# Attention outputs kept token-major in split fp32r, divided by the row sums on the way out of PSUM, and transposed afterwards

## The chip, the cores and the metric

One core of a Trainium2 chip runs the whole kernel. The metric is the device time in microseconds (us) of one execution, lower is better. The engines named below are TensorE (PE; its weight loads are shown apart as PEld), VectorE (DVE), ScalarE (ACT), GpSimd (POOL) and SyncE (SP), which issues most transfers.

## What is computed

One decoder block on 512 tokens of width 2048 in float32. Attention (16 heads of 64) and a state-space group share one input projection; each output is normalised, the two are concatenated and projected, and an MLP follows. With 512 tokens and key blocks of 256, every query sees all its past, so attention is plain causal attention with a distance penalty.

```python
h = rms_norm(x, norm1_gain)
q, k, v, u = split(h @ w_in)                    # 1024 columns each
attn = softmax(rms(q) @ rms(k).T * scale - slope * dist, causal) @ v
ssm = glu(gelu(s5(u)))
mixed = concat([rms_norm(attn, attn_out_gain), rms_norm(ssm, ssm_out_gain)])
x = x + mixed @ w_out
x = x + relu(rms_norm(x) @ w_ff1) ** 2 @ w_ff2
```

## The kernel before, in words

Every large product is made in fp32r (a float32 matmul that reads each operand once and at reduced precision), with both operands split into a high and a low part, so that it takes three matmuls: low by high, high by low, high by high. `panel` (lines 132 to 138) makes 512 columns: for each 128 rows of the weights, `split_w` makes the two parts of the weights (ACT copies the high part at line 110, DVE subtracts at line 111), and twelve matmuls of 512 columns go to four PSUM banks named `mm`. There is one set of four `mm` banks, so that the first matmul of a panel waits until the bank has been read out.

The stages follow one another in the program: the state-space part with its projection, q, k and v of heads 0 to 7, `attention(0)`, q, k and v of heads 8 to 15, `attention(1)`, two panels with `w_glu` (operand names `sh`, `sl`), four panels with the lower half of `w_out` (`zh`, `zl`, called the z panels below; their results are added to `x` at line 803), four panels with its upper half (`ah`, `al`, the a panels), and the MLP. The order on each engine is not the program's: a scheduler at build time places every instruction by priority and by its own estimate of times, and hands out buffers. Each engine then works through its list strictly in that order. So the pieces of `attention` stand between panel matmuls on PE, where the scheduler put them.

`attention` handles two heads at a time (`pr`), and for each of four query blocks `i` of 128 tokens and each head `e` one step, 64 steps in all:

- two matmuls make scores in the bank `sps` (lines 701, 702), of 128, 256, 384 or 512 columns for i = 0 to 3;
- DVE adds the distance term, takes the minimum and writes `sm` (line 706); ACT takes the exponential and the row sum (line 709); DVE inverts the sum (line 711) and POOL multiplies the probabilities by it (line 712);
- i + 1 transposes with `ident` put the probabilities into the bank `pps` (line 715), and ACT copies them to `pt` (line 717), in float32;
- i + 1 products in plain float32 (line 722) with 64 columns of `vv` as weights and 128 columns of `pt` moving; they fill `ops`, one head in its upper and one in its lower 64 partitions, so that the output stands feature by token. A float32 product of this kind appears in the trace as two instructions.

`sps`, `pps` and `ops` have one bank each. ACT copies `ops` to `oraw` once for each pair (line 726). Before the a panels, `oraw` is split into `ah`, `al` (lines 186, 187), its squares are made on ACT (line 816) and summed on POOL (line 817), and four small matmuls (line 779) add them over the partitions.

Of the kernel before, what the change touches and what calls it, by code (L numbers as in the profile page):

```python
# [8 lines left out]
F32 = mybir.dt.float32  # L9
F32R = mybir.dt.float32r  # L10
# [7 lines left out]
P = 128  # L18
# [3 lines left out]
DH = 64  # L22
# [23 lines left out]
def hybrid_block_kernel(ctx, tc, x, norm1_gain, w_in, q_norm_gain, k_norm_gain,  # L46
# [137 lines left out]
    def scaled_split(dh, dl, src, gain):  # L184

        S.activation(dh, src, AF.Copy, scale=gain)
        V.scalar_tensor_tensor(dl, src, gain, dh.bitcast(F32), op0=ALU.mult, op1=ALU.subtract)
# [498 lines left out]
        V.tensor_sub(klo[e][own], k, khh[own].bitcast(F32))  # L686
        return qhl, khh

    def attention(hf, qT, kT, vv, oraw):

        for pr in range(4):
            oT = aux("ops", "ops")
            slope = [2.0 ** (-8.0 * (hf * 8 + 2 * pr + e + 1) / H) for e in range(2)]
            parts = [head_parts(qT, kT, pr, e, 1.0 / slope[e]) for e in range(2)]
            for i in range(4):
                n = (i + 1) * P
                pts = []
                for e in range(2):
                    qhl, khh = parts[e]
                    sps = aux("sps", "sps")  # L700
                    PE.matmul(sps[:, :n], qhl[:, i * P:(i + 1) * P], khh[:, 0:n], start=True, stop=False)
                    PE.matmul(sps[:, :n], qhl[:, i * P:(i + 1) * P], klo[e][:, 0:n], start=False, stop=True)
                    sm = ap_.tile([P, 512], F32, name="sm", tag="sm", bufs=3)

                    mn = small.tile([P, 1], F32, name="mn", tag="mn")
                    V.tensor_tensor_reduce(sm[:, :n], sps[:, :n], dist[:, 512 - n:512], slope[e], 3e38,
                                           op0=ALU.add, op1=ALU.min, accum_out=mn)
                    rsum = small.tile([P, 1], F32, name="rsum", tag="rsum")
# [9 lines left out]
                    pts.append(pt)  # L718

                for b in range(i + 1):  # L720
                    for e in range(2):
# [6 lines left out]
    oraw = [ap_.tile([P, 4, 512], F32, name="oraw0")]  # L728
    attention(0, *qkv0, oraw[0])
    qkv1 = qkv(1, lambda n: ap_.tile([P, 4, 512], F32, name=n + "1"))  # L730


    sh, sl = [], []
# [6 lines left out]
            V.tensor_copy(h_, s0t(k))  # L740
            V.tensor_sub(l_, s0t(k), h_.bitcast(F32))

    oraw.append(page("oraw1"))
    attention(1, *qkv1, oraw[1])

    def sact(k):
        return sh[k // 4][:, k % 4, :], sl[k // 4][:, k % 4, :]
# [58 lines left out]
    open_banks(early, tx=3)  # L806
    ah = [page("ah0", F32R), page("ah1", F32R)]
    al = [page("al0", F32R), page("al1", F32R)]
    for k in range(8):
        o = oraw[k // 4][:, k % 4, :]  # L810
        scaled_split(ah[k // 4][:, k % 4, :], al[k // 4][:, k % 4, :], o, ga[:, k:k + 1])
        if k == 0:
            S.activation(rbc, o, AF.Square)
        else:
            oq = t2("oq")
            S.activation(oq, o, AF.Square)
            G.tensor_add(rbc, rbc, oq)
    rstda = row_rstd(rbc, "a")
    fin.close()

    def aact(k):
# [13 lines left out]
    for n in range(4):  # L835
        ps = panel(w_out, 0, 8, n * 512, aact, True)
        for m in range(4):
            with hi():
                xs = x1[m][:, n * 512:(n + 1) * 512]
                V.scalar_tensor_tensor(xs, ps[m], rstda[:, 2 * m:2 * m + 1], xs, op0=ALU.mult, op1=ALU.add)  # L840
# [240 lines left out]
```

## Time and profile before

| | |
|---|---|
| median of 3 runs | 2099.13 us (2098.68 to 2099.46) |
| the profiled execution | 2096.33 us, span of its instructions 2094.5 us |
| PE busy | 2061.8 us, 98% of the span |
| DVE, ACT, POOL busy | 1534.4, 829.1, 80.5 us |
| mean granted PE clock | 0.995 of full speed |

The profile covers one execution, from its first to its last instruction. A start-to-start distance of two PE rows is what an instruction costs PE when nothing is waited for; the duration that a row gives is longer, since matmuls overlap.

### The profile page before, as it was taken

The numbers are of one execution on the slowest core, as the hardware profiler recorded it, in microseconds if no ns is written. First come the engines' busy times: TensorE is split into PE (matmuls) and PEld (weight loads), VectorE is DVE, ScalarE is ACT, GpSimd is POOL, SyncE is SP. The second block draws the span as 40 slices with busy tenths as digits, with TensorE's granted clock in tenths as the row PEclk, the third lists the DMA queues.
The fourth block names the chain that finished last, engine by engine and source line by source line (L and its number), as shares of the span: only waits on it lengthen the run. The fifth ranks groups of instructions, "written<-read, shape, count | busy, mean of one in ns | idle before, by whom it ended". The sixth has DMA issues, their size and how long they took to land.

```text
span 2094.5 us, 26148 instructions
## 1 busy us (share of the span) xinstructions
PE 2061.8 (98%) x9881; PEld 1672.2 (80%) x9881; DVE 1534.4 (73%) x2659; ACT 829.1 (40%) x1349; POOL 80.5 (4%) x122
## 2 busy tenths in 40 slices
PE   8999999999999999999999999999999999999998
PEld 6777777776777888888888888888888888888887
DVE  6999994564773546677777777776877777777767
ACT  5244544455644333333333333333333333333332
POOL 1100000111331000000000000000000000000000
PEclk9999999999999999999999999999999999999999
DMA  6343332221233412333233333333333323333332
GB/s 194 119 124 96 93 101 81 79 73 61 82 110 105 162 37 69 117 105 98 93 111 101 101 114 108 94 97 111 101 101 111 110 91 100 111 101 101 109 108 95
DMA packets 149614, 213.51 MB, mean 102 GB/s; under 512 B 15672, under 2 KB 82320, under 8 KB 148976
## 3 DMA queue, kind: packets, MB, share of 16 engines
q1 hardware_dynamic: 136240, 201.36, 30.5%
q10 hardware_dynamic: 12416, 8.92, 1.4%
q0 software_dynamic: 832, 1.57, 0.3%
q8 instruction: 78, 1.28, 0.3%
q14 instruction: 48, 0.39, 0.1%
HBM read 204.54 MB, written 7.27 MB: 101 GB/s over the span
## 4 chain that ended last, share of the span: by engine, by line
PE 93%; DVE 5%; DMA 1%; ACT 1%; issue 1%; SPq 0%; POOL 0%; DVEq 0%; ACTq 0%; POOLq 0%
PE f L887 11%; PE f L888 11%; PE f L889 11%; PE g L983 9%; PE g L985 9%; PE g L981 9%; PE mm L132 7%; PE mm L133 7%; PE mm L134 7%; PE ops L722 1%; PE mm L136 1%; PE mm L138 1%; PE mm L137 1%; DMA x<-in_x_dram 1%; PE pps L715 1%; DVE wl L111 1%
## 5 line engine op out<-in xcount | busy, mean ns | idle before, releaser
L868 ACT CAST th<-w 128x1024 fp32r<-128x1024 f32 x349 | 361.7, 1053 | 642.6 <-PE g L985 467.4
L991 DVE TENSOR_TENSOR x<-x,g 128x512 f32<-128x512 f32 x434 | 293.6, 683 | 241.7 <-PE g L985 241.1
L869 DVE TENSOR_TENSOR tl<-w,th 128x1024 fp32r<-128x1024 f32 x349 | 425.6, 1220 | 61.1 <-ACT th L868 61.0
L887 PE MATMUL f<-h2h,tl 128*128 128x512 f32 x1024 | 398.6, 389 | 0.0
L888 PE MATMUL f<-h2l,th 128*128 128x512 f32 x1024 | 398.5, 389 | 0.0
L889 PE MATMUL f<-h2h,th 128*128 128x512 f32 x1024 | 398.4, 389 | 0.0
L983 PE MATMUL g<-tl,lf 128*128 128x512 f32 x868 | 337.9, 389 | 0.4 <-DVE tl L869 0.4
L985 PE MATMUL g<-th,lf 128*128 128x512 f32 x868 | 337.7, 389 | 0.0
L981 PE MATMUL g<-th,lf 128*128 128x512 f32 x868 | 320.0, 389 | 0.0
L889 PEld LDWEIGHTS f<-h2h,th 128*128 128x128 f32 x1024 | 192.2, 188 | 40.0
L887 PEld LDWEIGHTS f<-h2h,tl 128*128 128x128 f32 x1024 | 192.2, 188 | 39.9
L888 PEld LDWEIGHTS f<-h2l,th 128*128 128x128 f32 x1024 | 192.2, 188 | 39.8
L111 DVE TENSOR_TENSOR wl<-raw,wh 128x512 fp32r<-128x512 f32 x208 | 147.6, 711 | 96.8 <-ACT wh L110 96.2
L110 ACT CAST wh<-raw 128x512 fp32r<-128x512 f32 x208 | 127.8, 619 | 194.2 <-PE mm L134 117.3
L983 PEld LDWEIGHTS g<-tl,lf 128*128 128x128 f32 x868 | 162.9, 188 | 35.0 <-DVE tl L869 1.2
L981 PEld LDWEIGHTS g<-th,lf 128*128 128x128 f32 x868 | 162.9, 188 | 33.9
L985 PEld LDWEIGHTS g<-th,lf 128*128 128x128 f32 x868 | 162.9, 188 | 33.8
L133 PE MATMUL mm<-wl,xh 128*128 128x512 f32 x384 | 152.4, 397 | 0.0
L134 PE MATMUL mm<-wh,xh 128*128 128x512 f32 x384 | 152.1, 397 | 0.0
L132 PE MATMUL mm<-wh,xl 128*128 128x512 f32 x384 | 150.8, 399 | 0.7 <-ACT qs L628 0.4
L896 ACT ACTIVATE r<-r 128x512 f32<-128x512 f32 x64 | 40.0, 627 | 146.5 <-DVE r L895 146.5
L132 PEld LDWEIGHTS mm<-wh,xl 128*128 128x128 f32 x384 | 72.2, 188 | 16.6 <-issue 1.6
(350 smaller groups left out, 2552.4 us busy)
## 6 DMA issues: line engine op xcount, KB each, us to landing
w<-in_w_ff_dram SPq DMA_DIRECT2D x256, 512.0 KB, 3.8
raw<-in_w_in_dram SPq DMA_DIRECT2D x64, 512.0 KB, 3.7
raw<-in_w_out_dram SPq DMA_DIRECT2D x32, 512.0 KB, 3.6
x<-in_x_dram SPq DMA_DIRECT2D x7, 1024.0 KB, 10.3
m<-kp ACTq DMA_DIRECT2D x16, 256.0 KB, 3.3
raw<-in_w_glu_dram SPq DMA_DIRECT2D x8, 512.0 KB, 3.6
out_dram<-x SPq DMA_DIRECT2D x16, 256.0 KB, 2.2
ud<-sy ACTq DMA_DIRECT2D x8, 256.0 KB, 2.0
```

The source lines that it names most:

```text
L132: PE.matmul(ps[m], xl[:, ms], wh, start=st, stop=False)
L133: PE.matmul(ps[m], xh[:, ms], wl, start=False, stop=False)
L134: PE.matmul(ps[m], xh[:, ms], wh, start=False, stop=sp)
L868: S.copy(th, src)
L869: V.tensor_sub(tl, src, th.bitcast(F32))
L887: PE.matmul(ps[m], wl[:, k % 4, ms], xh_, start=k == 0, stop=False)
L888: PE.matmul(ps[m], wh[:, k % 4, ms], xl_, start=False, stop=False)
L889: PE.matmul(ps[m], wh[:, k % 4, ms], xh_, start=False, stop=k == 15)
L981: PE.matmul(ps[t], al_, th[:, q, :], start=first and q == 0, stop=False, skip_group_check=True)
L983: PE.matmul(ps[t], ah_, tl[:, q, :], start=False, stop=False, skip_group_check=True)
L985: PE.matmul(ps[t], ah_, th[:, q, :], start=False, stop=q == 1, skip_group_check=True)
L991: V.tensor_add(xs, xs, ps[t])
```

## The change: what it does

The products of probabilities and values change sides. The transposed probabilities become the weights (128 by 128) and the values move, so that the output stands token by feature. Both are split for fp32r: `pth`, `ptl` from the transposed probabilities (ACT copies, DVE subtracts), and `vhl`, which holds for each head the 64 high and the 64 low columns of the values side by side. Each product is then two matmuls: `pth` by all 128 columns, and `ptl` by the 64 high ones. The two halves are added when `ops` is read out, for two query blocks at a time, by three DVE operations that also multiply by the inverted row sums; the division by them before the transposes (POOL) is gone. The squares for the norm are taken on ACT with a row sum, and 32 transposes (`ot`), in the banks that `sps`, `pps` and `ops` leave, give the feature-by-token layout that the a panels need.

```diff
-    def attention(hf, qT, kT, vv, oraw):
+    def attention(hf, qT, kT, vv, o_sb):
...
+            vhl = ap_.tile([P, 4, 2, 2, DH], F32R, name="vhl", tag="vhl", bufs=1)
+            v = vv[:, :, pr * P:(pr + 1) * P].rearrange("p b (e d) -> p b e d", e=2)
+            S.copy(vhl[:, :, :, 0, :], v)
+            V.tensor_sub(vhl[:, :, :, 1, :], v, vhl[:, :, :, 0, :].bitcast(F32))
+            rsum = small.tile([P, 4, 2], F32, name="rsum", tag="rsum")
...
-                    S.activation(sm[:, :n], sm[:, :n], AF.Exp, bias=mn, scale=-1.0, accum_out=rsum)
-                    rinv = small.tile([P, 1], F32, name="rinv", tag="rinv")
-                    V.reciprocal(rinv, rsum)
-                    G.tensor_scalar(sm[:, :n], sm[:, :n], rinv, 0.0, op0=ALU.mult, op1=ALU.add)
+                    S.activation(sm[:, :n], sm[:, :n], AF.Exp, bias=mn, scale=-1.0,
+                                 accum_out=rsum[:, i, e:e + 1])
                     pps = aux("pps", "pps")
                     for b in range(i + 1):
                         PE.transpose(pps[:, b * P:(b + 1) * P], sm[:, b * P:(b + 1) * P], ident)
-                    pt = ap_.tile([P, 512], F32, name="pt", tag="pt", bufs=3)
-                    S.copy(pt[:, :n], pps[:, :n])
...
-                        PE.matmul(oT[e * DH:(e + 1) * DH, i * P:(i + 1) * P],
-                                  vv[:, b, pr * P + e * DH:pr * P + (e + 1) * DH],
-                                  pts[e][:, b * P:(b + 1) * P], start=b == 0, stop=b == i)
-            with hi():
-                S.copy(oraw[:, pr, :], oT)
+                    S.copy(pth[:, :n], pps[:, :n])
+                    V.tensor_sub(ptl[:, :n], pps[:, :n], pth[:, :n].bitcast(F32))
+                    o = ops[:, i % 2, e]
+                    for b in range(i + 1):
+                        bs = slice(b * P, (b + 1) * P)
+                        PE.matmul(o.rearrange("p l d -> p (l d)"), pth[:, bs],
+                                  vhl[:, b, e].rearrange("p l d -> p (l d)"), start=b == 0, stop=False,
+                                  skip_group_check=True)
+                        PE.matmul(o[:, 0], ptl[:, bs], vhl[:, b, e, 0], start=False, stop=b == i,
+                                  skip_group_check=True)
+                if i % 2:
+                    with hi():
+                        rinv = small.tile([P, 2, 2], F32, name="rinv", tag="rinv")
+                        V.reciprocal(rinv, rsum[:, i - 1:i + 1])
+                        d = o_sb[:, i - 1:i + 1, pr * P:(pr + 1) * P].rearrange("p i (e d) -> p i e d", e=2)
+                        V.tensor_copy(d, ops[:, :, :, 0])
+                        V.tensor_add(d, d, ops[:, :, :, 1])
+                        V.tensor_mul(d, d, bc(rinv, 3, DH))
...
-    qkv1 = qkv(1, lambda n: ap_.tile([P, 4, 512], F32, name=n + "1"))
+    qkv1 = qkv(1, lambda n: page(n) if n == "vv" else ap_.tile([P, 4, 512], F32, name=n + "1"))
...
+    for e in range(2):
+        for i in range(4):
+            junk = t2("junk")
+            S.activation(junk, o_sb[e][:, i, :], AF.Square, accum_out=ssa[:, i, e:e + 1])
...
     for k in range(8):
-        o = oraw[k // 4][:, k % 4, :]
-        scaled_split(ah[k // 4][:, k % 4, :], al[k // 4][:, k % 4, :], o, ga[:, k:k + 1])
...
-            G.tensor_add(rbc, rbc, oq)
-    rstda = row_rstd(rbc, "a")
+        ps = aux("ot", "tx")
+        for i in range(4):
+            PE.transpose(ps[:, i * P:(i + 1) * P], o_sb[k // 4][:, i, k % 4 * P:(k % 4 + 1) * P], ident)
+        scaled_split(ah[k // 4][:, k % 4, :], al[k // 4][:, k % 4, :], ps, ga[:, k:k + 1])
```

Where the pieces land is seen in the lists of the engines. First PE at the end of the z panels, before the change: the last z matmuls (weights `wh`, `wl`, moving `zh`, `zl`), the four small matmuls `rps`, and at once the first a panel (`ah`, `al`).

```order
L132 MATMUL mm_7002<-wh,zl_6183 128x512
L133 MATMUL mm_7002<-wl,zh_6181 128x512
L134 MATMUL mm_7002<-wh,zh_6181 128x512
L779 MATMUL rps<-ones,rbc 128x2 x4
L132 MATMUL mm_7214<-wh,al_7149 128x512
L133 MATMUL mm_7214<-wl,ah_7147 128x512
```

The last piece of attention stands 35 matmuls ahead of this place. PE at the same place in the changed kernel: the last z matmul, then pieces of attention alone.

```order
L134 MATMUL mm_7146<-wh,zh_6325 128x512
L726 MATMUL ops<-vhl,pth 128x128
L707 MATMUL sps<-khh,qhl 128x512
L708 MATMUL sps<-klo_3846,qhl 128x512
L729 MATMUL ops<-vhl,ptl 128x64
L726 MATMUL ops<-vhl,pth 128x128
L729 MATMUL ops<-vhl,ptl 128x64
L718 MATMUL pps<-ident,sm 128x128 x2
L726 MATMUL ops<-vhl,pth 128x128
```

From here 72 attention matmuls and transposes follow with no panel matmul among them, and at their end stand the last four transposes of a step, its eight products, sixteen of the new transposes `ot`, and the first a panel:

```order
L718 MATMUL pps<-ident,sm 128x128 x4
L726 MATMUL ops<-vhl,pth 128x128
L729 MATMUL ops<-vhl,ptl 128x64
L726 MATMUL ops<-vhl,pth 128x128
L729 MATMUL ops<-vhl,ptl 128x64
L726 MATMUL ops<-vhl,pth 128x128
L729 MATMUL ops<-vhl,ptl 128x64
L726 MATMUL ops<-vhl,pth 128x128
L729 MATMUL ops<-vhl,ptl 128x64
L833 MATMUL ot<-ident,o_3849 128x128 x16
L132 MATMUL mm_7388<-wh,al_7293 128x512
```

So the end of attention has moved from among the z panels to behind them. DVE at this place in the changed kernel (line 712 is the score operation, line 815 the z panel's read-out to `x`, lines 736 to 738 the read-out of `ops`):

```order
L815 SCALAR_TENSOR_TENSOR x_6703<-mm_7143,rstds,x_6703 128x512
L111 TENSOR_TENSOR wl<-raw,wh 128x512
L815 SCALAR_TENSOR_TENSOR x_6705<-mm_7144,rstds,x_6705 128x512
L815 SCALAR_TENSOR_TENSOR x_6707<-mm_7145,rstds,x_6707 128x512
L815 SCALAR_TENSOR_TENSOR x_6709<-mm_7146,rstds,x_6709 128x512
L111 TENSOR_TENSOR wl<-raw,wh 128x512
L712 ISA sm,mn<-sps,dist 128x512
L712 ISA mn 128x1
L722 TENSOR_TENSOR ptl<-pps,pth 128x256
L736 COPY o_5579<-ops 128x2x128
```

The scores of the last two steps thus stand behind the four read-outs of the last z panel. ACT at this place (line 714 is the exponential, line 721 makes `pth`, line 825 the squares):

```order
L721 CAST pth<-pps 128x384
L714 ACTIVATE sm,rsum<-sm,mn 128x512
L825 ACTIVATE junk,ssa<-o_5579 128x512 x2
L721 CAST pth<-pps 128x384
L721 CAST pth<-pps 128x512 x2
L825 ACTIVATE junk,ssa<-o_5579 128x512 x2
L186 ACTIVATE ah_7291<-ot,vt 128x512 x4
```

The last squares stand ahead of the first `ah` of the a panels. The second place is the end of the first `w_glu` panel, called stretch A in the prediction. PE there, before the change:

```order
L138 MATMUL mm_6187<-sh_5489,wh 128x512
L722 MATMUL ops<-pt,vv 64x128 x5
L715 MATMUL pps<-ident,sm 128x128 x4
L701 MATMUL sps<-khh,qhl 128x128
L702 MATMUL sps<-klo_3845,qhl 128x128
L701 MATMUL sps<-khh,qhl 128x128
L702 MATMUL sps<-klo_3846,qhl 128x128
L715 MATMUL pps<-ident,sm 128x128 x4
```

and in the changed kernel:

```order
L138 MATMUL mm_6331<-sh_5561,wh 128x512
L726 MATMUL ops<-vhl,pth 128x128
L707 MATMUL sps<-khh,qhl 128x384
L708 MATMUL sps<-klo_3846,qhl 128x384
L729 MATMUL ops<-vhl,ptl 128x64
L718 MATMUL pps<-ident,sm 128x128 x2
L707 MATMUL sps<-khh,qhl 128x512
L708 MATMUL sps<-klo_3845,qhl 128x512
L726 MATMUL ops<-vhl,pth 128x128
L729 MATMUL ops<-vhl,ptl 128x64
```

In both, a run of attention without a panel matmul begins here; it holds 12 score pairs in either list (29 transposes of `pps` and 33 products before, 27 and 25 in the changed one). A product now stands in two rows, and the transposes of the next step stand behind the products of the one before.

## Rows read from the trace of the kernel before

**Rows 1.** The page: busy time of PE and DVE, and the share of the chain that ended last.

```profile
PE 2061.8 (98%) x9881; PEld 1672.2 (80%) x9881; DVE 1534.4 (73%) x2659; ACT 829.1 (40%) x1349; POOL 80.5 (4%) x122
PE 93%; DVE 5%; DMA 1%; ACT 1%; issue 1%; SPq 0%; POOL 0%; DVEq 0%; ACTq 0%; POOLq 0%
```

**Rows 2.** Busy time by stretch: the stretch in us, its length, busy us of PE, PEld, DVE, ACT and POOL, the granted PE clock, and transfers. In order: stretch A, the gap after the first z panel (called stretch B), and the other three z panels.

```profile
507.90:531.70 23.80, 18.27 (x120) 12.33 (x120) 14.96 (x48) 13.24 (x36) 6.61 (x12) 0.91 0.07 23
...
591.90:598.90 7.00, 2.28 (x15) 1.21 (x13) 6.67 (x16) 3.52 (x8) 5.08 (x5) 0.76 0.03 11
598.90:682.30 83.40, 83.37 (x408) 65.54 (x409) 38.26 (x80) 33.64 (x67) 9.51 (x13) 0.98 0.30 98
```

**Rows 3.** PE by line and tile in the last three z panels (598.95 to 682.28 us): count, busy us, mean ns, idle us before.

```profile
L133 PE MATMUL mm<-wl,zh 128*128 128x512 f32 x96 | 38.7, 403 | 0.0
L722 PE MATMUL ops<-pt,vv 128*64 128x128 f32 x68 | 7.6, 285 | 0.0
L715 PE MATMUL pps<-ident,sm 128*128 128x128 f32 x31 | 5.4, 279 | 0.0
L702 PE MATMUL sps<-klo,qhl 128*128 128x512 f32 (+3 forms) x10 | 3.4, 335 | 0.0
```

**Rows 4.** PE in order of time inside these panels: start in us, duration, line and tile, shape, count.

```profile
612.04 0.39 PE L134 MATMUL mm<-wh,zh 128*128 128x512 f32 x1
...
614.54 0.39 PE L701 MATMUL sps<-khh,qhl 128*128 128x512 f32 x1
614.76 0.39 PE L702 MATMUL sps<-klo,qhl 128*128 128x512 f32 x1
615.08 0.87 PE L722 MATMUL ops<-pt,vv 128*64 128x128 f32 x10
615.88 0.50 PE L133 MATMUL mm<-wl,zh 128*128 128x512 f32 x1
616.22 0.39 PE L134 MATMUL mm<-wh,zh 128*128 128x512 f32 x1
...
616.68 0.60 PE L715 MATMUL pps<-ident,sm 128*128 128x128 f32 x4
617.03 0.48 PE L133 MATMUL mm<-wl,zh 128*128 128x512 f32 x1
617.35 0.39 PE L134 MATMUL mm<-wh,zh 128*128 128x512 f32 x1
...
620.32 0.39 PE L132 MATMUL mm<-wh,zl 128*128 128x512 f32 x1
620.54 0.22 PE L701 MATMUL sps<-khh,qhl 128*128 128x128 f32 x1
620.60 0.28 PE L702 MATMUL sps<-klo,qhl 128*128 128x128 f32 x1
620.71 0.45 PE L133 MATMUL mm<-wl,zh 128*128 128x512 f32 x1
621.00 0.39 PE L134 MATMUL mm<-wh,zh 128*128 128x512 f32 x1
```

**Rows 5.** PE in order of time around stretch A.

```profile
507.59 0.39 PE L138 MATMUL mm<-sh,wh 128*128 128x512 f32 x1
...
509.12 0.31 PE L701 MATMUL sps<-khh,qhl 128*128 128x128 f32 x1
509.27 0.27 PE L702 MATMUL sps<-klo,qhl 128*128 128x128 f32 x1
...
529.72 1.97 PE L722 MATMUL ops<-pt,vv 128*64 128x128 f32 x14
...
531.75 0.77 PE L136 MATMUL mm<-sh,wl 128*128 128x512 f32 x1
```

**Rows 6.** DVE, ACT and POOL between 330 and 680 us by line and shape: count, busy us, mean ns, idle us before.

```profile
L706 DVE CUSTOM_DVE_ANT_0 sm<-sps,dist 128x512 f32<-128x512 f32 x16 | 11.0, 690 | 2.5 <-PE sps L702 2.1
L706 DVE CUSTOM_DVE_ANT_0 sm<-sps,dist 128x128 f32<-128x128 f32 x16 | 4.6, 289 | 10.3 <-PE sps L702 10.0 <-issue 0.2
L803 DVE SCALAR_TENSOR_TENSOR x<-mm,rstds,x 128x512 f32<-128x512 f32 x12 | 8.5, 745 | 4.0 <-PE mm L134 3.9
L717 ACT COPY pt<-pps 128x512 f32<-128x512 f32 x16 | 9.3, 583 | 16.7 <-PE pps L715 16.7
L717 ACT COPY pt<-pps 128x128 f32<-128x128 f32 x16 | 4.2, 263 | 3.2 <-PE pps L715 3.0 <-ACT oraw L726 0.2
L816 ACT ACTIVATE oq<-oraw 128x512 f32<-128x512 f32 x7 | 4.2, 620 | 0.9 <-POOL rbc L817 0.9
L712 POOL TENSOR_SCALAR sm<-sm,rinv 128x256 f32<-128x256 f32 x16 | 8.7, 541 | 62.4 <-DVE rinv L711 51.9 <-DVE rs L182 4.0 <-DVE rw L180 3.3
```

**Rows 7.** PE in order of time at the end of the z panels.

```profile
682.29 0.95 PE L779 MATMUL rps<-ones,rbc 128*128 128x2 f32 x8
683.10 0.48 PE L132 MATMUL mm<-wh,al 128*128 128x512 f32 x1
```

**Rows 8.** PE and DVE in order of time in stretch B; the DVE rows are two like ones of 8 elements a partition.

```profile
598.93 0.79 PE L132 MATMUL mm<-wh,zl 128*128 128x512 f32 x1 [3.24 <-DVE x L803]
595.36 0.17 DVE L179 TENSOR_TENSOR rw<-rstds 128x8 f32<-128x8 f32 x1
595.56 1.12 DVE L180 TENSOR_TENSOR rw<-rw,sss 128x8 f32<-128x8 f32 x1
```

More of the change, by code (lines that the diff above doesn't have):

```diff
@@ L687, in head_parts @@
         return qhl, khh
-    def attention(hf, qT, kT, vv, oraw):
+    def attention(hf, qT, kT, vv, o_sb):
         for pr in range(4):
-            oT = aux("ops", "ops")
             slope = [2.0 ** (-8.0 * (hf * 8 + 2 * pr + e + 1) / H) for e in range(2)]
             parts = [head_parts(qT, kT, pr, e, 1.0 / slope[e]) for e in range(2)]
+            vhl = ap_.tile([P, 4, 2, 2, DH], F32R, name="vhl", tag="vhl", bufs=1)
[3 more added lines that the diff above has]
+            rsum = small.tile([P, 4, 2], F32, name="rsum", tag="rsum")
             for i in range(4):
                 n = (i + 1) * P
-                pts = []
+                if i % 2 == 0:
+                    ops = aux("ops", "ops").rearrange("p (i e l d) -> p i e l d", i=2, e=2, l=2)
                 for e in range(2):
@@ L707, in attention @@
                                            op0=ALU.add, op1=ALU.min, accum_out=mn)
-                    rsum = small.tile([P, 1], F32, name="rsum", tag="rsum")
-                    S.activation(sm[:, :n], sm[:, :n], AF.Exp, bias=mn, scale=-1.0, accum_out=rsum)
-                    rinv = small.tile([P, 1], F32, name="rinv", tag="rinv")
-                    V.reciprocal(rinv, rsum)
-                    G.tensor_scalar(sm[:, :n], sm[:, :n], rinv, 0.0, op0=ALU.mult, op1=ALU.add)
+                    S.activation(sm[:, :n], sm[:, :n], AF.Exp, bias=mn, scale=-1.0,
+                                 accum_out=rsum[:, i, e:e + 1])
                     pps = aux("pps", "pps")
@@ L715, in attention @@
                         PE.transpose(pps[:, b * P:(b + 1) * P], sm[:, b * P:(b + 1) * P], ident)
-                    pt = ap_.tile([P, 512], F32, name="pt", tag="pt", bufs=3)
-                    S.copy(pt[:, :n], pps[:, :n])
-                    pts.append(pt)
-                for b in range(i + 1):
-                    for e in range(2):
-                        PE.matmul(oT[e * DH:(e + 1) * DH, i * P:(i + 1) * P],
-                                  vv[:, b, pr * P + e * DH:pr * P + (e + 1) * DH],
-                                  pts[e][:, b * P:(b + 1) * P], start=b == 0, stop=b == i)
-            with hi():
-                S.copy(oraw[:, pr, :], oT)
-    oraw = [ap_.tile([P, 4, 512], F32, name="oraw0")]
-    attention(0, *qkv0, oraw[0])
-    qkv1 = qkv(1, lambda n: ap_.tile([P, 4, 512], F32, name=n + "1"))
+                    pth = ap_.tile([P, 512], F32R, name="pth", tag="pth", bufs=2)
+                    ptl = ap_.tile([P, 512], F32R, name="ptl", tag="ptl", bufs=2)
+                    S.copy(pth[:, :n], pps[:, :n])
[16 more added lines that the diff above has]
+                        V.tensor_mul(d, d, bc(rinv, 3, DH))
+    o_sb = [ap_.tile([P, 4, 512], F32, name="o0")]
+    attention(0, *qkv0, o_sb[0])
+    qkv1 = qkv(1, lambda n: page(n) if n == "vv" else ap_.tile([P, 4, 512], F32, name=n + "1"))
     sh, sl = [], []
@@ L741, in hybrid_block_kernel @@
             V.tensor_sub(l_, s0t(k), h_.bitcast(F32))
-    oraw.append(page("oraw1"))
-    attention(1, *qkv1, oraw[1])
+    o_sb.append(page("o1"))
+    attention(1, *qkv1, o_sb[1])
     def sact(k):
@@ L808, in hybrid_block_kernel @@
     al = [page("al0", F32R), page("al1", F32R)]
-    for k in range(8):
-        o = oraw[k // 4][:, k % 4, :]
-        scaled_split(ah[k // 4][:, k % 4, :], al[k // 4][:, k % 4, :], o, ga[:, k:k + 1])
[L812 to L816, printed above, removed]
-            G.tensor_add(rbc, rbc, oq)
-    rstda = row_rstd(rbc, "a")
+    ssa = const.tile([P, 4, 2], F32, name="ssa")
+    for e in range(2):
+        for i in range(4):
+            junk = t2("junk")
+            S.activation(junk, o_sb[e][:, i, :], AF.Square, accum_out=ssa[:, i, e:e + 1])
+    ssr = const.tile([P, 4], F32, name="ssr")
+    V.tensor_reduce(ssr, ssa, axis=AX.X, op=ALU.add)
+    rstda = const.tile([P, 4], F32, name="rstda")
+    rsqrt_mean(rstda, ssr, 1024, [P, 4])
+    for k in range(8):
+        ps = aux("ot", "tx")
+        for i in range(4):
+            PE.transpose(ps[:, i * P:(i + 1) * P], o_sb[k // 4][:, i, k % 4 * P:(k % 4 + 1) * P], ident)
+        scaled_split(ah[k // 4][:, k % 4, :], al[k // 4][:, k % 4, :], ps, ga[:, k:k + 1])
     fin.close()
@@ L839, in hybrid_block_kernel @@
                 xs = x1[m][:, n * 512:(n + 1) * 512]
-                V.scalar_tensor_tensor(xs, ps[m], rstda[:, 2 * m:2 * m + 1], xs, op0=ALU.mult, op1=ALU.add)
+                V.scalar_tensor_tensor(xs, ps[m], rstda[:, m:m + 1], xs, op0=ALU.mult, op1=ALU.add)
             S.activation(rbc, xs, AF.Square, accum_out=ssq2[:, m, n:n + 1])
```

## The prediction, made before the changed kernel ran

> **What bounds the kernel now.** I read the busy times and the chain that ended last first [rows 1]: PE is busy for 98% of the span and holds 93% of the chain. So an edit counts in two ways: by the PE time that it adds or takes where PE never waits, and by the waits at the few places where PE has nothing else to do. The table by stretch shows both kinds [rows 2]. In the last three z panels PE is busy for 83.37 of 83.40 us: whatever DVE and ACT do for attention there is hidden, and a step costs only its PE time. In stretch A PE is busy for 18.27 of 23.80 us, without a panel matmul: it lies open. In stretch B PE works 2.28 of 7.00 us, while DVE is busy for 6.67. The passage from the last z panel to the first a panel costs .8 us, 682.29 to 683.10 [rows 7].
>
> The prices on PE come from the list in order of time [rows 4]. From 612.04 to 614.54 lie eleven matmuls of 512 columns: .227 each. Between the starts at 614.76 and 616.22 stand two such matmuls and five float32 products: 1.46 − .45 = 1.0, .20 a product in a run of five. From 616.68 to 617.35 stand four transposes and a panel matmul: .44, .11 a transpose. The small score pair at 620.54, two fp32r matmuls of 128 columns, takes 621.00 − 620.54 − .227 = .23, thus about .115 each.
>
> **The change, part by part.** I sum only two kinds of places: hidden stretches by PE time, and the three open places by walking through the waits. The counts are those of the lists of instructions, before and after.
>
> *A hidden product.* The 83.4 us of the last z panels hold 3 × 96 panel matmuls (65.4 us) [rows 3]; the granted clock of .98 [rows 2] costs about 1.6; 31 transposes take 3.5, ten score pairs of mixed width (.45 for 512 columns, .23 for 128) about 3.3. 9.6 us are left for the 34 products (68 rows [rows 3]): .285 each. That is more than the .20 of the run of five, since most products stand alone between fp32r matmuls. After the change a product is two small fp32r matmuls. The trace has no such row with 64 columns; the nearest is the small score pair, .115 a matmul. Since the weights of both are 128 columns, as in that pair and in a transpose (.11), I take .109 for either, so .218 a product. The bounds are .06 (620.54 to 620.60 [rows 4]) and .15 (509.12 to 509.27 [rows 5], on an idle PE).
>
> The Trainium skill, page "TensorE: Matmul & The Clock Gate", section "Back-to-back issue gap", gives about 81 ns for a matmul of 128 columns in a stream of weight loads and matmuls. By that figure the hidden products would cost 109 × 2 × .028 = 6.1 us less than in my sum, which goes by the row, where the small pair took .115 a matmul.
>
> *Hidden attention.* Before, 123 of the 160 products, 126 transposes and 51 of the 64 score pairs stand in hidden stretches; after, 109, 107 and 47, since more lies at the open places. 123 × .285 − 109 × .218 = 11.3 us saved, 19 transposes 2.3, four pairs 1.3: **−14.9 us**.
>
> *A step at an open place.* The bank `pps` is single, and now the next step's transposes stand on PE behind the products of the one before. So a step is a loop: transposes, `pth` on ACT, `ptl` on DVE, products, then the next. `pth` costs what the copies at L717 cost, .263 to .583 for 128 to 512 columns [rows 6]. `ptl` reads PSUM and one more operand, as the score operation does: .289 to .690 [rows 6]. With transposes of .11, products of .218 and about .75 for the first transpose, product and hand-offs, i = 0 takes 1.29, and each step of i adds .11 + .107 + .134 + .218 = .57: 1.86, 2.42 and 2.99 for i = 1, 2, 3.
>
> *Stretch A.* The changed list has four steps of i = 1 there and two each of i = 0, 2 and 3: 7.4 + 2.6 + 4.8 + 6.0 = 20.8, and half-finished steps at both ends, 2.4 by the same prices: 23.3. DVE's share grows from 14.96 us [rows 2] to about 22 (scores, `ptl`, read-outs of `ops`, and the parts of heads and `wl` that stand among them), so it often comes late: 23.3 to 28. I take 26.5 against 23.8: **+2.7**.
>
> *Stretch B.* Its DVE chain (row sums, four read-outs) stays, with fewer of POOL's additions beside it: two like small operations took .17 and 1.12 us [rows 8]. The Trainium skill, page "SBUF — State Buffer", section "SBUF: two separate sides", says that VectorE with two SBUF inputs and a GpSimd operation that reads SBUF lock each other out of one port pair; the 1.12 agrees with it, though no row shows the lock itself. My sum takes no gain from this, since more `ptl` operations are queued in between: 8.1 against 7.2: **+.9**.
>
> *The tail.* This is the largest term. The last attention steps now stand behind the z panels, and nothing is beside them. Counting from the end of the last z matmul: DVE has the read-outs (.745 each [rows 6]) and two `wl` of like size ahead of the scores of the last two steps; the first of the four banks is done 2.0 us before the end, so they finish near 6 × .745 − 2.0 = 2.5. The half-done steps with i = 1 end near 3.6. Two steps of i = 2 and two of i = 3 follow, 4.8 + 6.0, to 14.4. The squares, .62 each [rows 6], stand ahead of a `pth` on ACT: with the delay beyond their cover of .5 and the last hand-offs, 15.3. Three read-out operations of `ops` at about .42 (256 elements, between .289 and .690): 16.6. The last two squares, 1.2: 17.9 with hand-off. `ah` .71 (a square's .62 and a hand-off) and `al` .75 (as a read-out): 19.35. But the first a panel stands behind all sixteen transposes `ot` in PE's list, and these need a bank that the first `al` sets free: four transposes and hand-off, .6: 20.0. PE's own work in this is 18 products, 16 transposes, two pairs and 16 `ot`, 8.6 us; over 11 us are waits. Against .8: **+19.2**. Bounds: 17 if the squares and read-outs never stand in the way, 24 at the lower clock, where fourteen product rows took 1.97 us and a panel matmul .77 in its row [rows 5].
>
> *Clock.* Stretch B shows a granted clock of .76 and A .91 already [rows 2], 1.2 GHz in part. The tail will add a fall, and the first z panels or a panels pay for it, while B, with more in it, may pay less: **+.5** (−1.4 to +3).
>
> *Nothing:* the weight copies and transfers of the MLP that move past the squares (PE has three k of a panel, 2.7 us each, ahead of them); POOL's work, 80.5 us in all [rows 1], waited for by few; `vhl`, one copy and one subtraction a pair behind panels. Without this cover they would cost their own .4 to .7 a pair.
>
> **Sum:** −14.9 + 2.7 + .9 + 19.2 + .5 = +8.4 us. The profiled execution took 2096.3, the median of the runs is 2099.1, 2.8 above; the sum against the first gives 2104.7, and in the terms of the median **2107.5 us**.
>
> **The rivals.**
>
> 1. *Slower weight loads.* If a small matmul costs .15 in the stream, 109 × 2 × .041 = 8.9 us more: 2116. For it: the isolated pair [rows 5]; against it: the pair in the stream [rows 4].
>
> 2. *Faster ones.* With .06 a matmul (the gap between the two rows at 620.5 [rows 4]), 109 × 2 × .049 = 10.7 us less; with .085, half way to my value, 5.3: 2097 to 2102, no difference that can be told. For it: the second matmul of that pair began after .06. Against it: the pair as a whole took .23, and .11 a transpose.
>
> 3. *The other side: the open places shrink.* Each step loses the reciprocal and POOL's multiplication (.541 for 256 columns [rows 6]) from its chain of waits, and DVE is freed of what stood at 1.12 instead of .17 [rows 8]. If two steps then overlap, with products of one beside the `ptl` of the other, A falls to DVE's present busy time, 15.0 us, B to 4, and the tail to 14 (4.8 + 6.0 overlapped to 5, and the fixed 9): −14.9 − 8.8 − 3.2 + 13.2 + .5 = −13.2, 2086. It decides from the point at which A, B and tail together need less than 23.8 + 7.2 + .8 + 14.9 − .5 = 46.2 us; I forecast 54.6. For it: POOL's place in the chain. Against it: one `pps` bank and PE's fixed list, in which the next transposes stand behind the products, and DVE's greater load.
>
> **How the numbers follow.** 0.2%, 4.2 us, is about what a measurement of this kernel can tell from no change: 2094.9 to 2103.3 is "same". The forecast (slower) has .62, slower weight loads .12, faster ones .16 (same), shrinking places .10 (faster). So slower .74, same .16, faster .10. The tail's bounds (−3 to +4), A's (−3 to +1.5) and the clock (−2 to +2.5) give the likeliest case 2101 to 2114; the lower end, 2100, reaches into the faster weight loads and the upper, 2118, takes in the slower ones.
>
> **What would show it.** In the changed trace: the gap between the last z and first a panel matmul, 20 us (17 to 24), with PE busy for some 9 and waiting for `pth`, `ptl` and `ah`; in the hidden stretches pairs of L726 and L729 at .22, and three z panels shorter by some 8%; stretch A 26 us with DVE busy for most of it; no POOL row of L712. The prediction is wrong if the tail comes under 12 us, if a pair in the stream costs .15 or .30, or if the attention steps in A overlap.

## The result and the profile after

The changed kernel takes 2122.71 us (median of 4, 2121.71 to 2123.16) against 2098.90 for the kernel before: ratio 1.0119, 95% interval 1.0107 to 1.0130, or 23.8 us slower. The forecast was 8.4 us slower, 2107.5, with a range of 2100 to 2118: the direction held, the size did not. The profiled execution has a span of 2121.0 us, 26.5 more than before.

The page of the changed kernel, the two lines that answer to [rows 1]:

```profile
PE 2075.6 (98%) x9905; PEld 1705.9 (80%) x9905; DVE 1566.1 (74%) x2731; ACT 833.7 (39%) x1359; POOL 30.2 (1%) x51
PE 87%; DVE 9%; DMA 2%; ACT 1%; issue 1%; ACTq 0%; SPq 0%; DVEq 0%
```

PE's share of the chain falls from 93% to 87% and DVE's rises from 5% to 9%: more of the span is spent waiting. Busy time by stretch of the changed kernel (columns as in [rows 2]): the first `w_glu` panel, stretch A, up to stretch B, stretch B, the other z panels, the tail.

```profile
474.86:500.02 25.16, 25.16 (x128) 21.33 (x127) 14.88 (x33) 8.05 (x19) 0.00 (x0) 1.00 0.27 84
500.02:536.40 36.38, 25.77 (x101) 19.74 (x100) 22.46 (x61) 15.53 (x41) 0.00 (x0) 0.60 0.05 15
536.40:591.10 54.70, 54.70 (x268) 46.21 (x268) 46.58 (x79) 35.59 (x67) 12.61 (x7) 0.96 0.38 138
591.10:603.94 12.84, 6.85 (x35) 5.90 (x33) 12.11 (x39) 4.63 (x11) 0.00 (x0) 0.68 0.21 69
603.94:683.69 79.75, 79.75 (x401) 67.62 (x400) 42.58 (x95) 29.50 (x66) 0.00 (x0) 0.99 0.22 73
683.69:707.15 23.46, 17.07 (x74) 13.87 (x73) 10.85 (x28) 9.26 (x21) 0.00 (x0) 0.59 0.37 119
```

Between the last and the next panel matmul, the three open places take 36.4, 12.8 and 23.5 us, where the kernel before had 24.2, 7.4 and 1.0. That is 40.1 us more. All PE work hidden behind panels has shrunk: the first `w_glu` panel begins 6.0 us earlier (474.86 against 480.85), the panels between there and the z panels take 4.2 us less outside A, the z panels 5.8 less outside B and the tail, 16.0 in all. (Each of these is read from one execution of either kernel; A begins between 498.1 and 500.7 us in the ten runs of the changed form, so they are good to a us or two.) Behind the tail 2.4 us are lost, of which the clock of the first a panel (.97 over 22.9 us) is .7; the rest was not traced to a cause. −16.0 + 40.1 + 2.4 = 26.5.

What stands out is the clock: it was granted at .60 in A, .68 in B and .59 in the tail; A of the kernel before had .91 [rows 2]. Stretch A from its second step on, PE's transposes (each begins a step, and their count is i + 1) and the longest waits for scores:

```profile
503.22 0.44 PE L718 MATMUL pps<-ident,sm 128*128 128x128 f32 x2
...
505.81 0.50 PE L707 MATMUL sps<-khh,qhl 128*128 128x512 f32 x1 [1.30 <-DVE mn L712]
...
506.62 0.55 PE L718 MATMUL pps<-ident,sm 128*128 128x128 f32 x3
...
509.78 0.48 PE L707 MATMUL sps<-khh,qhl 128*128 128x128 f32 x1 [2.60 <-DVE mn L712]
...
511.67 0.90 PE L718 MATMUL pps<-ident,sm 128*128 128x128 f32 x3
...
514.87 1.11 PE L718 MATMUL pps<-ident,sm 128*128 128x128 f32 x4
...
518.96 1.11 PE L718 MATMUL pps<-ident,sm 128*128 128x128 f32 x4
...
523.05 0.47 PE L718 MATMUL pps<-ident,sm 128*128 128x128 f32 x1
...
525.53 0.47 PE L718 MATMUL pps<-ident,sm 128*128 128x128 f32 x1
...
527.54 0.67 PE L718 MATMUL pps<-ident,sm 128*128 128x128 f32 x2
...
530.45 0.69 PE L718 MATMUL pps<-ident,sm 128*128 128x128 f32 x2
...
534.37 0.90 PE L718 MATMUL pps<-ident,sm 128*128 128x128 f32 x3
```

The steps at 503.22 and 506.62 take 3.40 and 5.05 us, where the forecast's loop gave 1.86 and 2.42. What DVE does meanwhile:

```profile
502.73 0.41 DVE L684 CAST khh<-kT 64x512 fp32r<-64x512 f32 x1
503.17 0.42 DVE L685 CAST khh<-kT 64x512 fp32r<-64x512 f32 x1
503.62 0.68 DVE L686 TENSOR_TENSOR klo<-kT,khh 64x512 fp32r<-64x512 f32 x1
504.33 0.69 DVE L683 SCALAR_TENSOR_TENSOR qhl<-qT,qhl 64x512 fp32r<-64x512 f32 x1
505.05 0.69 DVE L712 CUSTOM_DVE_ANT_0 sm<-sps,dist 128x512 f32<-128x512 f32 x1
```

The operands of the next heads stand ahead of the score's read-out, and PE waits for the bank. The granted clock falls to .50, 1.2 GHz, at 507.1 (.53 from 507 to 508), and PE's work from 509.78 on shows it: three transposes last .90 instead of .55, and steps of i = 3 take 4.09 us instead of 2.99, of i = 1 2.91 instead of 1.86.

### The profile page after: what moved, and what is told of

Read it like the earlier page. It is cut to its first block, busy times and chain, and to the rows that moved or that the text cites. A ratio compares the mean times of both kernels' runs of the same rounds, so it can differ in the third digit from the quotient of the medians.

```text
span 2121.0 us, 26094 instructions
## 1 busy us (share of the span) xinstructions
PE 2075.6 (98%) x9905; PEld 1705.9 (80%) x9905; DVE 1566.1 (74%) x2731; ACT 833.7 (39%) x1359; POOL 30.2 (1%) x51
## 4 chain that ended last, share of the span: by engine, by line
PE 87%; DVE 9%; DMA 2%; ACT 1%; issue 1%; ACTq 0%; SPq 0%; DVEq 0%
PE f L903 11%; PE f L905 11%; PE f L904 11%; PE g L999 9%; PE g L1001 9%; PE g L997 9%; PE mm L132 5%; PE mm L134 5%; PE mm L133 5%; PE mm L137 2%; PE mm L136 2%; PE mm L138 2%; DVE wl L111 1%; PE pps L718 1%; PE ops L726 1%
```

## The experiments

Three theories for the missing 15 us. **Clock:** the forecast's steps were right, but at an open place PE falls to 1.2 GHz. **DVE's list:** the read-outs come late, at any clock. **Serial loop:** one `pps` bank, with the next transposes behind the products, leaves PE idle. fill2, fill4, fill8, khh_pool_b and the two before_less were run once, and are read by their profiles; the others give medians. Gains are taken against the 2122.71 of the changed kernel. It was not run again beside them, and the kernel before, which was, took 2097.3 to 2097.4 there instead of 2098.9; so each gain may be some 1.5 us too large.

**Matmuls that do nothing, in stretch A.** Eight of them stand behind each score pair of heads 8 and 9 (four in fill4, two in fill2):

```diff
+                    if (hf, pr) == (1, 0):
+                        fill = ax("fill")
+                        for _ in range(8):
+                            PE.matmul(fill[:, :512], qhl[:, i * P:(i + 1) * P], khh[:, :512], start=True, stop=True)
```

> The changed kernel, with eight matmuls of 512 columns added behind each of the eight score pairs of heads 8 and 9, into a bank that nobody reads. The lists of the attention instructions stay as they are; the eight steps lie in stretch A from its 10th us on. The added work is 64 x .227 = 14.5 us at the high clock level. Theory 1 (clock): stretch A took 36.4 us instead of 26.5 because PE's waits in its first 10 us let the clock fall and everything after ran at 1.2 GHz (granted .50). The added matmuls stand where PE waits for pth and ptl; the clock comes back inside A, and A takes 26 to 32 us in spite of the added work. Theory 2 (DVE's list): A is as long as DVE's scores, head parts and read-outs make it at any clock; A stays at 36 or gets longer. If the clock does not come back, the fillers alone take 64 x .43 = 27.5 us and A takes 55 to 60.

> As fill8, with four added matmuls a step, 32 x .227 = 7.3 us. Theory 1: if that is enough to bring the clock back, A takes 25 to 30 us; theory 2: 36 or more; with no clock gained, 36.4 + 32 x .43 - 3 = 47.

> The changed kernel with two added matmuls of 512 columns a step in stretch A (fill4 had four, and A took 35.4 us with the clock at 1.00 in its second quarter; fill8 41.5). If two hold the clock up: 16 x .227 = 3.6 us of work for a loss of up to 7 us, A 30 to 33 us. If they do not: 16 x .43 = 6.9 us at the low clock, partly in waits, A 38 to 41.

Measured: A took 41.5 us with eight, 35.4 with four, 37.9 with two, against 36.4 with none (36.4 to 36.7 in three runs with its list unchanged). The whole took 2128.46, 2120.67 and 2122.47 us. Busy time of A as a whole with four, and PE's transposes in it:

```profile
499.73:535.13 35.40, 27.41 (x133) 21.71 (x131) 22.44 (x61) 15.53 (x41) 0.00 (x0) 0.81 0.04 16
```

```profile
515.81 0.66 PE L722 MATMUL pps<-ident,sm 128*128 128x128 f32 x4
...
519.22 0.66 PE L722 MATMUL pps<-ident,sm 128*128 128x128 f32 x4
...
522.13 0.33 PE L722 MATMUL pps<-ident,sm 128*128 128x128 f32 x1
...
524.42 0.33 PE L722 MATMUL pps<-ident,sm 128*128 128x128 f32 x1
```

A step of i = 3 takes 3.41 and 2.91 us with four or more added matmuls inside it, where it took 4.09 without: 7.3 us of added work cost less than nothing, since the granted clock of A rose from .60 to .81 (.89 with eight, .63 with two). That is the clock theory for the middle of A. It is not all of A: neither four nor eight brought it to the 25 to 32 us expected, and the 41.5 of fill8 lie on the side that its expectation gave to DVE's list, at a clock of .99 or 1.00 from 516 on. With four the clock was down again at the end (.50 from 526 on), and the waits for DVE stayed in both.

**The open place elsewhere.** One small matmul behind the last score pairs of heads 6 and 7 makes the scheduler place the pieces otherwise:

```diff
+                    if (hf, pr, i) == (0, 3, 3):
+                        fill = ax("fill")
+                        for _ in range(1):
+                            PE.matmul(fill[:, :128], qhl[:, i * P:(i + 1) * P], khh[:, :128], start=True, stop=True)
```

> The changed kernel with one matmul of 128 columns added, twice, behind the score pairs of the last step of heads 6 and 7, into a bank that nobody reads. It moves the list: 3 score pairs, 5 transposes and 8 product matmuls are left in stretch A instead of 11, 27 and 50; stretch B and the tail keep theirs. If stretch A is what went wrong: 36.4 us there become some 5, and the PE work moved under panels costs 2.8 + 2.4 + 4.6 = 9.8 us: 21 us faster than the changed kernel, about 2101. If the wait only moves to another place, it stays within 5 us of 2122.7.

Measured: 2119.86 us, 2.9 less than the changed kernel, not 21. My reading of the list was too narrow: A did shrink to 6.3 us, but the bank of the added matmul is the one that `qt` uses, and an open place of 25.5 us with 8 score pairs, 20 transposes and 40 product matmuls appeared between two panels of the projection. So the wait only moved, the second outcome expected. It shows the steps at both clock levels:

```profile
417.60 0.66 PE L722 MATMUL pps<-ident,sm 128*128 128x128 f32 x4
...
420.52 0.66 PE L722 MATMUL pps<-ident,sm 128*128 128x128 f32 x4
...
424.14 0.47 PE L722 MATMUL pps<-ident,sm 128*128 128x128 f32 x1
...
426.63 0.47 PE L722 MATMUL pps<-ident,sm 128*128 128x128 f32 x1
...
428.64 0.67 PE L722 MATMUL pps<-ident,sm 128*128 128x128 f32 x2
...
431.55 0.69 PE L722 MATMUL pps<-ident,sm 128*128 128x128 f32 x2
```

At the high clock the first step of i = 3 takes 2.92 us (forecast 2.99); the clock falls during the next, and then i = 0 takes 2.49 and 2.01, i = 1 2.91: to .02 us what the like steps of A took. So it is not stretch A as a place that loses the clock: this loop lost it here too, 6 us after the last panel matmul. The 6.3 us that are left of A stay at the high clock (its three transposes at 528.71 last .55 us).

**DVE's list.** In parts_pool2 POOL (`G`) makes the two copies of the keys and their low part for heads 8 to 11; in khh_pool_b it makes the two copies alone, for heads 12 and 13. The edit of the first:

```diff
-    def head_parts(qT, kT, pr, e, inv):
+    def head_parts(qT, kT, pr, e, inv, V=V):
...
-        V.scalar_tensor_tensor(qhl[oth], q, inv, qhl[own].bitcast(F32), op0=ALU.mult, op1=ALU.subtract)
+        nc.vector.scalar_tensor_tensor(qhl[oth], q, inv, qhl[own].bitcast(F32), op0=ALU.mult, op1=ALU.subtract)
         V.tensor_copy(khh[own], k)
         V.tensor_copy(khh[oth], k)
...
-            parts = [head_parts(qT, kT, pr, e, 1.0 / slope[e]) for e in range(2)]
+            parts = [head_parts(qT, kT, pr, e, 1.0 / slope[e], G if (hf, pr) in ((1, 0), (1, 1)) else V) for e in range(2)]
```

> The changed kernel, where for heads 8 to 11 the two copies of the keys and the low part of the keys (L684 to L686) are made by POOL instead of DVE; PE's list in stretch A, stretch B and the tail keeps its counts. In the changed kernel the steps of stretch A that start at 503.22 and 506.62 take 3.40 and 5.04 us against 1.86 and 2.42 by the formula, with waits for the score's read-out, and these parts stand in DVE's list ahead of it; after them the clock is at .50. Theory (DVE's list starts it, the clock spreads it): with the parts off DVE these two steps come to within .7 us of the formula, the clock stays up for longer, and A falls from 36.4 to 27 to 31 us; the whole to 2113 to 2118. Rival (the clock falls anyway since the steps themselves leave PE idle for half the time): the two steps get shorter by 3 us in sum, the clock still falls, A is 33 and the whole 2119. Rival (POOL and DVE hinder each other, or POOL is slower than the gap): A stays at 36 or more.

> The changed kernel with the two copies of the keys of heads 12 and 13 on POOL; PE's list keeps its counts at all three open places. In stretch B (12.84 us) DVE was busy for 12.07 of 12.8 us, and PE waited 4.76 us for a score's read-out, with two of these copies (.84 us), the row-sum chain and two weight splits ahead of it in DVE's list. If DVE's list is what makes B long: B falls by .8 to 1.2 us, to 11.6 to 12.0. If the low clock alone made it long: 12.8.

Measured: parts_pool2 takes 2119.29 us, A 34.3. The step of 5.05 us falls to 4.06, the other stays at 3.45, PE's waits for scores in A fall from 7.2 to 3.6 us, and the clock is down all the same, from 503.8 on. That is nearest to the second outcome, the clock falls anyway, though the two steps lose .9 us in sum and not 3. In khh_pool_b the whole stays where it was (2122.45 us), and stretch B falls from 12.84 to 11.17 us, more than the .8 to 1.2 expected, with DVE still busy for 10.74 of it:

```profile
592.31:603.48 11.17, 6.48 (x34) 5.98 (x33) 10.74 (x33) 3.57 (x9) 1.78 (x2) 0.73 0.21 77
```

DVE's list inside B lost six operations and 1.4 us, not the two copies alone, and B lost 1.7. That fits DVE's list as what makes B long, and not the low clock alone (12.8 expected). In the changed kernel PE's longest wait at an open place stands there, behind such operands, two `wl` and the chain of the row sums:

```profile
596.71 0.69 DVE L686 TENSOR_TENSOR klo<-kT,khh 64x512 fp32r<-64x512 f32 x1
...
598.18 0.47 PE L707 MATMUL sps<-khh,qhl 128*128 128x128 f32 x1 [4.76 <-DVE mn L712]
```

**Less work in the kernel before.** Most products of heads 6 to 9 are left out (heads 8 and 9 alone in before_less1):

```diff
-                for b in range(i + 1):
+                for b in (range(i + 1) if not ((hf, pr) in ((0, 3), (1, 0))) else [i]):
...
-                                  pts[e][:, b * P:(b + 1) * P], start=b == 0, stop=b == i)
+                                  pts[e][:, b * P:(b + 1) * P], start=b == 0 or ((hf, pr) in ((0, 3), (1, 0))), stop=b == i)
```

> The kernel before with most products of heads 6 to 9 left out (of the i + 1 products of a step only the last one, so that these heads' output is not the reference's). Stretch A keeps its 12 score pairs and 29 transposes, but holds 11 products instead of 33: 22 x .20 = 4.4 us less of PE work at the high clock. Theory (the clock follows PE's work at an open place): in the kernel before the long float32 products kept PE busy for 77% of A and the clock at .91; with less work the clock falls to .50 early in A, and A takes 24 to 28 us, as long as before or longer, with a granted clock under .75. Rival (the clock plays no part; A is its chain of waits and its work): A falls to 19 to 22 us.

> The same for heads 8 and 9 alone (their output is not the reference's): 21 products in stretch A, 2.4 us less work. Theory: clock lower than .91, A at 24 us or above. Rival: A at 21 to 23 us, clock as before.

Measured: A took 21.4 and 22.6 us (24.2 before), with a granted clock of .88 and .90. The theory that the long float32 products kept the clock up did not come out, and the rival's numbers hold; but the test is a mild one, since A got shorter with the work: PE was busy for 16.07 of its 21.38 us, 75% against 77% before. The clock fell 16 and 18 us after the last panel matmul instead of 20. What the two lists differ in besides: in the kernel before, the next scores and often the next transposes stand ahead of the products of the step before. That this keeps PE's waits short is a reading of the list, and it leads to the serial loop:

```diff
-                    pps = aux("pps", "pps")
+                    pps = ax("pps2") if (hf, pr) == (1, 0) and e == 1 else aux("pps", "pps")
```

> The changed kernel with a second bank for the transposed probabilities in every other step of heads 8 and 9 (the bank that qt used). PE's list in stretch A keeps its 11 score pairs and 50 product matmuls (30 transposes for 27); in the last third of A the next transposes stand ahead of the products of the step before. Stretch B is left with 1 pair, 4 transposes and 6 product matmuls instead of 3, 10 and 15; the tail's list is the same. If the serial loop is what makes PE idle: the steps that alternate banks take 1.5 us instead of 2.0 to 2.9, A falls by 3 to 5 us, B by 4 to 6: 2112 to 2116. If the clock is down by then and rules alone: A 35 to 37, B 9: 2119.

Measured: 2112.51 us, 10.2 less than the changed kernel; A 32.5 us, B 3.6 (and 3.0 a little ahead of it). PE's transposes in A:

```profile
522.75 0.47 PE L718 MATMUL pps<-ident,sm 128*128 128x128 f32 x1
...
525.62 0.65 PE L718 MATMUL pps<-ident,sm 128*128 128x128 f32 x2
...
526.13 0.69 PE L718 MATMUL pps<-ident,sm 128*128 128x128 f32 x2
...
528.71 0.86 PE L718 MATMUL pps<-ident,sm 128*128 128x128 f32 x3
...
529.86 0.90 PE L718 MATMUL pps<-ident,sm 128*128 128x128 f32 x3
```

From the second step of i = 0 to the end of the last products of i = 1 it takes 7.1 us (522.75 to 529.86), where the same three steps took 8.8 in the changed kernel (525.53 to 534.37); two steps now begin .51 us apart (525.62 and 526.13), and the transposes at 528.71 stand ahead of the products that end these steps. The clock stays at .50 (from 504.2 to 531), so the bank's gain is one of order, not of clock. Attention is then ahead when B comes, and B is all but gone.

**The tail.** Half of the transposes `ot` are made ahead of the closing of the attention banks:

```diff
+    for k in range(4):
+        ps = ax("ot0")
+        for i in range(4):
+            PE.transpose(ps[:, i * P:(i + 1) * P], o_sb[0][:, i, k * P:(k + 1) * P], ident)
+        scaled_split(ah[0][:, k, :], al[0][:, k, :], ps, ga[:, k:k + 1])
```

> The changed kernel with the transposes ot of heads 0 to 7 made from the bank that qt used, ahead of the closing of the attention banks. The list has the first 48 matmuls of the first a panel (10.9 us) behind the z panels at once, among the last attention steps; 28 product matmuls, 11 transposes and the other ot follow behind them. If the tail is only a lack of panel work: 10.9 us covered, 2112. If it is also the low clock (granted .59 in those 23.4 us), the chain gets shorter too: 2107 to 2110. If the first a matmuls wait for al, or the squares hold up ACT: 2120.

> parts_pool2 and ot_early together. If the two places are independent, the gains add: ot_early gained 5.6 us, so 5.6 under parts_pool2: 2107 to 2112. If the early transposes in stretch B (12 of the 16 stand there) cost what they save, the same as parts_pool2.

> second_pps, parts_pool2 and ot_early together; the gains of parts_pool2 and ot_early alone were 3.4 and 5.6 us, and together 7.6. If the three are independent, 7.6 and what second_pps gains: 2106 to 2111. The kernel before stays ahead, since A (some 30 us) and the tail's chain of the last four steps are left.

Measured: 2117.10 us for ot_early, 5.6 gained, between the expected outcomes; half of the cover of 10.9 us came out. The first a panel starts without a gap, but 16.1 us stay open after its 48th matmul, at .61 of the clock: attention's pieces stand between the panel matmuls, and wait for them too. pool_ot_early takes 2115.15, above the 2107 to 2112 expected of independent places (7.6 gained, 9.0 by addition, no clear difference where a gain is good to 1.5 us); three_together takes 2104.25 (ratio to the kernel before 1.0034, 1.0021 to 1.0047): 18.5 gained, and 7.6 + 10.2 = 17.8. So the remedies add, as far as these runs can tell. Against the kernel before beside it, three_together is 6.9 us slower instead of 23.8: the three undo about seven tenths of the loss.

**One half of the heads as before.** Heads 8 to 15 go through the function of the kernel before, named `attention_old`, with ot_early's edit; its `pt` has two buffers here instead of three:

```diff
-    attention(1, *qkv1, o_sb[1])
+    attention_old(1, *qkv1, o_sb[1])
```

> Heads 0 to 7 as in the changed kernel, heads 8 to 15 as in the kernel before (probabilities scaled by POOL, float32 products, output feature by token), the transposes ot of heads 0 to 7 made early. It keeps the hidden gain of the first half and has neither the tail nor an open stretch B in its list; stretch A holds 15 score pairs, 39 transposes and 29 products of both kinds. The first half's hidden gain was 6.0 us at the first w_glu panel (474.9 against 480.9). If hidden products are what the change is worth and the open places are what it costs: 6 us gained, 2 for the sixteen ot, A of some 30 to 35 us instead of 24.2, B of 7.4 us gone: 2095 to 2102, within the measurement of the kernel before. If the open places follow the new form of products only, A falls under 27 and the whole under 2094. If the hidden gain was no gain of the products, 2105 or more.

Measured: 2102.28 us (ratio 1.0021, 1.0011 to 1.0030), just above the 2095 to 2102 expected. The first `w_glu` panel begins at 473.96, .9 us ahead of the changed kernel's, so the hidden gain is that of the first half's form. Stretch A takes 40.6 us for its 15 pairs:

```profile
499.12:539.72 40.60, 32.16 (x150) 22.89 (x148) 24.49 (x74) 19.08 (x53) 5.93 (x11) 0.66 0.04 14
```

A's 16.4 us more than before take back the hidden gain. A does not separate the two forms: its steps up to 522.45 are of the new form, and the clock fell among them (.50 from 504.4 on); it held at .50 through the first steps of the old form and was back at 1.00 from 532 on, among their float32 products.

## Why the forecast was wrong in size, step by step

**The hidden product was right.** In the changed kernel:

```profile
499.25 0.22 PE L726 MATMUL ops<-vhl,pth 128*128 128x128 f32 x1
499.31 0.24 PE L729 MATMUL ops<-vhl,ptl 128*128 128x64 f32 x1
499.39 0.33 PE L718 MATMUL pps<-ident,sm 128*128 128x128 f32 x1
499.47 0.48 PE L136 MATMUL mm<-sh,wl 128*128 128x512 f32 x1
...
499.79 0.40 PE L137 MATMUL mm<-sl,wh 128*128 128x512 f32 x1
```

499.79 − 499.25 − .227 = .31 for two products' matmuls and a transpose, .10 each; in fill8, at the high clock, six such matmuls took .64 us from start to start of what followed (519.42 to 520.06), .107 each. I took .109. The term came to −16.0 us against −14.9, so neither rival of slower or faster weight loads holds. (Small slips in the working change little: 9.6 us over 34 products are .282 each, not .285; 19 transposes at .11 are 2.1, not 2.3; the changed kernel's A holds 11 score pairs in the trace, not 12, so that 48 and not 47 are hidden; and the pair at 509.12 stood behind four transposes, not on an idle PE.) The figure of .081 that the Trainium skill gives ("TensorE: Matmul & The Clock Gate", "Back-to-back issue gap") is not reached here: the measured .10 to .107 decides.

**The step that failed is the step at an open place: its price was that of the high clock, and DVE's part in it was set too low.** By the trace the three places cost 40.1 us more than before, where the forecast had 22.8: A is short by 9.5, B by 4.5, the tail by 3.3. For the clock the forecast had "+.5" and the 24 at the tail's upper bound, although [rows 2] and [rows 5] showed the low level in A and B. At the high clock the formula holds: other runs show steps there of i = 3 (2.92 us in one_dummy, forecast 2.99), of i = 2 (ot_early, 2.34 against 2.42) and of i = 1 (fill8, behind the last added matmul, 1.88 against 1.86):

```profile
699.45 0.55 PE L718 MATMUL pps<-ident,sm 128*128 128x128 f32 x3
...
701.79 0.89 PE L718 MATMUL pps<-ident,sm 128*128 128x128 f32 x4
```

```profile
533.84 0.41 PE L722 MATMUL pps<-ident,sm 128*128 128x128 f32 x2
...
535.72 0.44 PE L722 MATMUL pps<-ident,sm 128*128 128x128 f32 x2
```

At the low clock the seven steps of A from 511.67 to 534.37 took 22.7 us, by the formula 14.7. Against their likes at the high clock, one step of i = 2 lost .9 us (3.20), two of i = 3 lost 1.2 each (4.09) and the first of i = 1 lost 1.0 (2.91): 4.2 us are shown to be the clock's. Not so the first step of i = 0: in fill4 it took 2.29 us at the high clock (522.13 to 524.42), waiting for DVE, and 2.48 here. The last of i = 1, with the operands of the next heads in it, took 3.50 in fill8 (535.72 to 539.22) and 3.92 here. The other step of i = 0 has no like; it took .7 more than the formula. So about 5 of the 8.0 us are the clock's and about 3 are waits for DVE; the two overlap, and the split is no sharper than that. In the tail my walk held nearly everywhere: the half-done steps end at 3.6 us after the last z matmul as forecast, the read-outs take 1.3, the squares 1.2. The four steps do not: from 687.50 to the end of the last product at 702.2 they take 14.7 us instead of 11.7 (3.6 to 15.3), all but the transposes of the first at the low clock (.50 from 689 on). That is the distance between the 20.0 us forecast and the 23.2 measured, near the bound of 24 that was given for the lower clock. In the first of the four the products wait 1.22 us, to the read-out of `ops` (L737); the squares, for which I allowed .5, held up nothing.

```profile
687.50 0.55 PE L718 MATMUL pps<-ident,sm 128*128 128x128 f32 x3
...
690.72 0.90 PE L718 MATMUL pps<-ident,sm 128*128 128x128 f32 x3
...
693.93 1.11 PE L718 MATMUL pps<-ident,sm 128*128 128x128 f32 x4
...
698.01 1.11 PE L718 MATMUL pps<-ident,sm 128*128 128x128 f32 x4
...
701.87 0.36 PE L729 MATMUL ops<-vhl,ptl 128*128 128x64 f32 x1
...
703.29 2.79 PE L833 MATMUL ot<-ident,o 128*128 128x128 f32 x12 [1.06 <-DVE o L737]
```

**DVE's lateness was undersized.** I allowed A 3.2 us for it. The first four steps, from the transposes at 499.39 to 511.67, took 12.3 us against 7.4 by the formula; with the 3 or so in the later ones that makes about 8. (The end of the 5.05 us step lies at the low clock already.) DVE's own load was right (22.46 us, forecast "about 22"); what I missed is that it comes in lumps, 2.2 us of operands for a head ahead of one read-out. B is the same: 12.11 us of DVE work in 12.84, in 39 operations where the kernel before had 16; I forecast 8.1 us. The shorter small operations that I did not count on did come, with POOL idle in B: the like of the 1.12 us one (L180 [rows 8]) takes .17 or less each time. The added work outweighs it.

**The other side,** shrinking places, would have needed two steps in flight. The list has one bank and one step at a time, as the forecast objected; second_pps shows that two steps do overlap once there is a second bank.

What stays open is what makes the clock fall. In the kernel before it stayed at 1.00 for the first 19 us of A (.50 from 528 on); in the ten runs of the changed form it fell 4 to 7 us after the last panel matmul of A. Neither fewer waits (parts_pool2) nor less work in the kernel before (before_less) turned it, and no run sets the two forms of a step side by side in the same list.

## What to carry to other kernels

A step that is hidden costs its PE time, and a step at an open place costs its whole loop. In this kernel each of the three open places (and the one of one_dummy) spent most of its time at the low clock or behind DVE's list: price such a step from rows at 1.2 GHz too, walk through the other engine's list, and ask of a change first how many steps it leaves open. Here 16 us were gained behind panels and 40 lost at the open places, 22 of them since the end of attention moved behind the z panels, which the forecast had seen. A second bank for the piece that closes the loop was worth more (10.2 us) than moving work off the busy engine (3.4).

## What was not expected of the hardware

Added matmuls that nobody reads, 7.3 us of them, made an open place 1.0 us shorter, in one run, as the granted clock rose from .60 to .81; with 3.6 us of them it rose to .63 only and the place became 1.5 us longer. In parts_pool2 POOL made the copies of the keys in .61 us each and the subtraction in 1.56 on average, where DVE took .42 and .69 in A; in khh_pool_b the two copies took 1.14 and .64.
